# Two normalisation helpers of a three-block layer stack: the weight is multiplied before the statistics, the scaling after them is one operation a half

## The chip, the cores and the metric

The kernel runs on one core of a Trainium2 chip. The metric is the device time of one execution in microseconds, from several executions of the same program, of which the median is given. One execution was also recorded by the hardware profiler, and every row below is from that one. PE is the TensorE matmul engine (PEld its weight loads), DVE is VectorE, ACT is ScalarE, POOL is GpSimd, and SP issues DMAs.

## The reference, cut to what matters

A sequence of 512 positions with 1024 features goes through two layers of one kind and one of another. Each layer normalises, multiplies by weights, adds to the residual, and does so again for its feed-forward half:

```python
def rms_norm(x, g):
    y = x * rsqrt(mean(x * x, axis=-1, keepdims=True) + EPS)
    return y * g

def hybrid_layer(x, ...):              # twice
    u = rms_norm(x, g_mix_pre) @ w_in
    mix = concat([attention(u), conv(u), retention(u)]) @ w_out
    x = x + rms_norm(mix, g_mix_post)
    f = square(relu(rms_norm(x, g_mlp_pre) @ w_up)) @ w_down
    return x + rms_norm(f, g_mlp_post)

def second_block(h, ...):              # once
    proj = rms_norm(h, norm1_gain) @ w_in          # attention and a state-space branch
    h = h + (gated sum of both branches) @ w_out
    return h + glu_conv(rms_norm(h, norm2_gain) @ w_up) @ w_down
```

The row statistic of a norm is one number per position, the weight g one number per feature.

## The kernel before, in words

The 512 positions are four tiles t of 128; a tile's residual row block X[t] is two halves h of 128x512 floats in SBUF. All matrix products are made from high and low parts in fp32r (names ending in hi and lo), three matmuls for each. Weights come as one stream of 512 KB pieces (tile wraw); each is split by a cast to whi (ACT) and a subtraction to wlo (POOL or DVE).

Two helpers make the norms. `post_update(t, srcs, X, gpost)` takes the two halves of a product (from PSUM, or from the SBUF accumulators acc), squares each on ACT with an accumulated sum into the small tile st, adds the two sums on DVE, raises to the power -0.5 on POOL, and then on DVE, for each half, writes tmp = src * st * gain and adds tmp to X. `pre_norm(t, X, gpre)` takes the same statistic of X and writes, on DVE, hs = X * st * gain. `to_hT` then transposes hs on PE (matmuls with the identity cm), and a cast on ACT (hhi) and a subtraction on DVE (hlo) make the left operand of the next stage. In the trace hs and tmp both bear the name t, the weights gain, and the squares' unused output junk.

There are six sites. At the start, `pre_norm` is made for four tiles of the input. Then, twice, `finish` (after w_out: the first half's product p0[t] lies in PSUM, the second half is computed in a loop over t) and `finish_mlp` (after w_down: both halves are added into acc in a loop over t) each do `post_update`, `pre_norm` and the next tile's products in turn. Last, the second block's w_out loop does `pre_norm` alone. So there are 24 calls of `pre_norm` and 16 of `post_update`, 8 on PSUM halves and 8 on acc.

Behind each site the next stage begins with `f_split`: four products on the first 256 columns (tiles 0 and 1), then the same four on the other 256; `mid_start` puts the transposes of tiles 2 and 3 among the first ones. The next stage therefore can't begin before tile 1 is through its norms, transposes and split.

The order of the instructions is written out ahead of time. Every call is recorded by `Trace.add` with its dependences and a due time; `Trace.order` simulates the five engines with fixed costs (`cost`), takes on each engine the ready operation with the earliest due time within a window, gives out buffers (55 SBUF tiles of 128x512, four and four PSUM banks), chooses between engines for casts (`copy`) and subtractions (`sub`), and `issue` then emits that order. Its costs know nothing of one engine waiting for another's SBUF access. Each engine then executes in that order, so an instruction that waits holds all behind it on its engine. Since all is emitted from line 642, rows bear L642 and are told apart by tile names.

Of the kernel before, what the change touches and what calls it, by code (L numbers as in the profile page):

```python
# [13 lines left out]
AF = mybir.ActivationFunctionType  # L14
ALU = mybir.AluOpType
# [793 lines left out]
class Builder:  # L809
# [149 lines left out]
    def post_update(self, t, srcs, X, gpost):  # L959
        nc = self.nc  # L960
        st = self.st()
        for h in range(2):
            nc.scalar.activation(self.junk(), srcs[h], AF.Square, scale=1.0 / 32, accum_out=st[:, h:h + 1])
        nc.vector.scalar_tensor_tensor(st[:, 2:3], st[:, 0:1], EPS, st[:, 1:2], op0=ALU.add, op1=ALU.add)
        nc.gpsimd.tensor_tensor(st[:, 3:4], st[:, 2:3], self.mhalf[:, :1], op=ALU.pow)
        for h in range(2):
            tmp = self.s2()
            nc.vector.scalar_tensor_tensor(tmp, srcs[h], st[:, 3:4], gpost[h], op0=ALU.mult, op1=ALU.mult)
            nc.vector.tensor_tensor(X[t][h], X[t][h], tmp, op=ALU.add)

    def pre_norm(self, t, X, gpre):
        nc = self.nc
        st = self.st()
        for h in range(2):
            nc.scalar.activation(self.junk(), X[t][h], AF.Square, scale=1.0 / 32, accum_out=st[:, h:h + 1])
        nc.vector.scalar_tensor_tensor(st[:, 2:3], st[:, 0:1], EPS, st[:, 1:2], op0=ALU.add, op1=ALU.add)
        nc.gpsimd.tensor_tensor(st[:, 3:4], st[:, 2:3], self.mhalf[:, :1], op=ALU.pow)
        hs = []
        for h in range(2):
            tmp = self.s2()  # L980
            nc.vector.scalar_tensor_tensor(tmp, X[t][h], st[:, 3:4], gpre[h], op0=ALU.mult, op1=ALU.mult)
            hs.append(tmp)
        return hs

    def to_hT(self, t, hs):
# [1102 lines left out]
```

## Time and profile before

| | |
|---|---|
| median of 3 runs | 2135.91 us (2134.16 to 2139.28) |
| the profiled execution's own time | 2135.72 us |
| its span, first to last instruction | 2134.0 us |
| PE busy | 2036.2 us (95%) |
| DVE busy | 1362.7 us (64%) |
| ACT busy | 931.8 us (44%) |
| POOL busy | 727.8 us (34%) |
| mean granted TensorE clock | 0.990 |

Busy shares are means over the whole run. In a timeline row the number in square brackets is how long the engine was idle just before that row, and what ended the idle time; xN says that N instructions of one kind are merged in a row, and the time is then that of all N. PEclk in a table by stretches is the mean granted clock there, 1.00 being 2.4 GHz and 0.50 being 1.2 GHz.

### The profile page before, as it was taken

The numbers are of one execution on the slowest core, as the hardware profiler recorded it, in microseconds if no ns is written. First come the engines' busy times: TensorE is split into PE (matmuls) and PEld (weight loads), VectorE is DVE, ScalarE is ACT, GpSimd is POOL, SyncE is SP. The second block draws the span as 40 slices with busy tenths as digits, with TensorE's granted clock in tenths as the row PEclk, the third lists the DMA queues.
The fourth block names the chain that finished last, engine by engine and source line by source line (L and its number), as shares of the span: only waits on it lengthen the run. The fifth ranks groups of instructions, "written<-read, shape, count | busy, mean of one in ns | idle before, by whom it ended". The sixth has DMA issues, their size and how long they took to land. (4 is left out here: it accounts for less than half of the span.)

```text
span 2134.0 us, 27037 instructions
## 1 busy us (share of the span) xinstructions
PE 2036.2 (95%) x9964; PEld 1709.2 (80%) x9964; DVE 1362.7 (64%) x2127; ACT 931.8 (44%) x1527; POOL 727.8 (34%) x858
## 2 busy tenths in 40 slices
PE   7999889999999998899999998999999999999999
PEld 7987788778888977688888887677777788888887
DVE  5998795444457998563445473379888546655545
ACT  3377544222234376543233244457568224333322
POOL 3662367970004662300000035854553431000000
PEclk9999999999999999999999999999999999999999
DMA  5423333333242423222333354322324423333322
GB/s 181 129 60 119 109 103 130 111 117 99 79 126 90 129 72 116 79 90 89 98 90 108 99 186 139 91 85 65 98 82 146 164 88 100 99 99 99 97 81 79
DMA packets 85556, 225.16 MB, mean 106 GB/s; under 512 B 10416, under 2 KB 20400, under 8 KB 85424
## 3 DMA queue, kind: packets, MB, share of 16 engines
q1 hardware_dynamic: 85424, 223.43, 32.9%
q8 instruction: 79, 1.29, 0.3%
q14 instruction: 53, 0.43, 0.1%
HBM read 204.25 MB, written 19.14 MB: 105 GB/s over the span
## 5 line engine op out<-in xcount | busy, mean ns | idle before, releaser
L642 POOL TENSOR_TENSOR wlo<-wraw,whi 128x1024 fp32r<-128x1024 f32 (+1 forms) x156 | 367.1, 2361 | 1066.9 <-ACT whi L642 865.7
L642 ACT CAST whi<-wraw 128x1024 fp32r<-128x1024 f32 (+1 forms) x323 | 330.8, 1031 | 702.7 <-PE ps L642 617.8
L642 PE MATMUL ps<-hhi,whi 128*128 128x512 f32 (+1 forms) x1488 | 502.7, 367 | 8.7 <-DVE acc L642 2.8
L642 PE MATMUL ps<-hlo,whi 128*128 128x512 f32 (+1 forms) x1488 | 501.7, 367 | 6.8 <-DVE hlo L642 6.8
L642 PE MATMUL ps<-hhi,wlo 128*128 128x512 f32 (+1 forms) x1488 | 501.4, 366 | 0.4 <-DVE wlo L642 0.3
L642 PEld LDWEIGHTS ps<-hhi,whi 128*128 128x128 f32 x1488 | 273.5, 191 | 52.7 <-issue 5.1
L642 PEld LDWEIGHTS ps<-hlo,whi 128*128 128x128 f32 x1488 | 273.8, 192 | 49.3 <-DVE hlo L642 7.9
L642 PEld LDWEIGHTS ps<-hhi,wlo 128*128 128x128 f32 x1488 | 273.4, 191 | 43.4 <-DVE wlo L642 1.4
L642 DVE TENSOR_TENSOR wlo<-wraw,whi 128x1024 fp32r<-128x1024 f32 x178 | 224.6, 1263 | 109.2 <-ACT whi L642 109.1
L642 PE MATMUL ps<-whi,fhi 128*128 128x512 f32 x688 | 249.0, 391 | 5.1 <-DVE acc L642 2.8
L642 PE MATMUL ps<-whi,flo 128*128 128x512 f32 x688 | 249.3, 390 | 0.0
L642 PE MATMUL ps<-wlo,fhi 128*128 128x512 f32 x688 | 249.2, 391 | 0.0
L642 DVE TENSOR_TENSOR acc<-ps,acc 128x512 f32<-128x512 f32 x112 | 76.5, 687 | 153.0 <-PE ps L642 153.0
L642 PE MATMUL ps<-wlo,hhi 128*128 128x384 f32 (+1 forms) x448 | 157.6, 371 | 3.8 <-POOL wlo L642 3.8
L642 PE MATMUL ps<-whi,hhi 128*128 128x384 f32 (+1 forms) x448 | 155.7, 371 | 0.9 <-ACT whi L642 0.7
L642 PEld LDWEIGHTS ps<-whi,fhi 128*128 128x128 f32 x688 | 129.5, 188 | 32.6 <-DVE acc L642 3.2
L642 PE MATMUL ps<-whi,hlo 128*128 128x384 f32 (+1 forms) x448 | 155.3, 370 | 0.0
L642 PEld LDWEIGHTS ps<-whi,flo 128*128 128x128 f32 x688 | 129.7, 189 | 27.1
L642 PEld LDWEIGHTS ps<-wlo,fhi 128*128 128x128 f32 x688 | 129.8, 189 | 26.9
L642 POOL TENSOR_TENSOR st<-st,mhalf 128x1 f32<-128x1 f32 (+1 forms) x56 | 54.8, 980 | 194.0 <-DVE st L642 192.0
L642 DVE TENSOR_SCALAR t<-ps 128x512 f32<-128x512 f32 x64 | 44.1, 690 | 87.9 <-PE ps L642 87.9
L642 DVE TENSOR_TENSOR X<-ps,X 128x512 f32<-128x512 f32 x56 | 38.6, 689 | 91.7 <-PE ps L642 91.7
(249 smaller groups left out, 3247.5 us busy)
## 6 DMA issues: line engine op xcount, KB each, us to landing
wraw<-in_wst SPq DMA_DIRECT2D x302, 512.0 KB, 3.5
wraw<-in_wst SPq DMA_DIRECT2D x32, 384.0 KB, 3.1
gain<-in_gains SPq DMA_DIRECT2D x20, 256.0 KB, 4.3
X<-in_x SPq DMA_DIRECT2D x16, 256.0 KB, 5.4
xd<-X SPq DMA_DIRECT2D x16, 256.0 KB, 2.0
X<-xd SPq DMA_DIRECT2D x16, 256.0 KB, 5.5
gated<-t SPq DMA_DIRECT2D x16, 256.0 KB, 2.1
gate<-gated SPq DMA_DIRECT2D x16, 256.0 KB, 3.6
```

The source lines that it names most:

```text
L642: getattr(getattr(self.nc, e), m)(*[r(x) for x in op.args], **{k: r(v) for k, v in op.kw.items()})
```

## The change

In `post_update` each source half is multiplied by its weight into a new tile sg before the statistic, and after it one DVE operation a half adds sg * st to X. In `pre_norm` the weight is multiplied into hs before the statistic on DVE, and after it ACT scales hs in place by st.

```diff
     def post_update(self, t, srcs, X, gpost):
         nc = self.nc
         st = self.st()
+        sg = []
         for h in range(2):
+            sg.append(self.s2(name="sg"))
+            nc.vector.tensor_tensor(sg[h], srcs[h], gpost[h], op=ALU.mult)
             nc.scalar.activation(self.junk(), srcs[h], AF.Square, ...)
         nc.vector.scalar_tensor_tensor(st[:, 2:3], ...)
         nc.gpsimd.tensor_tensor(st[:, 3:4], ..., op=ALU.pow)
         for h in range(2):
-            tmp = self.s2()
-            nc.vector.scalar_tensor_tensor(tmp, srcs[h], st[:, 3:4], gpost[h], op0=ALU.mult, op1=ALU.mult)
-            nc.vector.tensor_tensor(X[t][h], X[t][h], tmp, op=ALU.add)
+            nc.vector.scalar_tensor_tensor(X[t][h], sg[h], st[:, 3:4], X[t][h], op0=ALU.mult, op1=ALU.add)

     def pre_norm(self, t, X, gpre):
         nc = self.nc
         st = self.st()
+        hs = []
         for h in range(2):
+            hs.append(self.s2())
+            nc.vector.tensor_tensor(hs[h], X[t][h], gpre[h], op=ALU.mult)
             nc.scalar.activation(self.junk(), X[t][h], AF.Square, ...)
         nc.vector.scalar_tensor_tensor(st[:, 2:3], ...)
         nc.gpsimd.tensor_tensor(st[:, 3:4], ..., op=ALU.pow)
-        hs = []
         for h in range(2):
-            tmp = self.s2()
-            nc.vector.scalar_tensor_tensor(tmp, X[t][h], st[:, 3:4], gpre[h], op0=ALU.mult, op1=ALU.mult)
-            hs.append(tmp)
+            nc.scalar.activation(hs[h], hs[h], AF.Copy, scale=st[:, 3:4])
         return hs
```

## Rows read from the trace of the kernel before

**Rows 1.** The page's first part: busy time, share of the span, instructions.
```profile
PE 2036.2 (95%) x9964; PEld 1709.2 (80%) x9964; DVE 1362.7 (64%) x2127; ACT 931.8 (44%) x1527; POOL 727.8 (34%) x858
```
**Rows 2.** Waits of PE, whole run: total us, times, longest us.
```profile
PE ps L642 <- DVE t L642: 19.6, 14, 2.8
PE ps L642 <- DVE hlo L642: 6.8, 5, 2.4
PE ps L642 <- ACT hhi L642: 1.9, 2, 1.5
```
**Rows 3.** Stretches around five sites: length, busy us of each engine, clock, DMA.
```profile
0.00:27.00 27.00, 13.94 (x90) 12.97 (x91) 16.57 (x22) 13.40 (x27) 13.12 (x12) 1.00 0.80 283
252.00:296.00 44.00, 35.13 (x205) 31.39 (x204) 38.34 (x74) 16.15 (x36) 24.30 (x22) 0.88 0.35 113
640.00:660.00 20.00, 16.66 (x97) 14.64 (x95) 18.82 (x23) 11.28 (x24) 12.87 (x8) 0.91 0.31 100
895.00:915.00 20.00, 14.39 (x82) 12.21 (x81) 19.58 (x28) 10.42 (x22) 8.89 (x7) 0.91 0.36 106
1260.00:1280.00 20.00, 16.60 (x125) 15.28 (x124) 18.36 (x27) 13.46 (x30) 14.22 (x9) 1.00 0.74 244
```
**Rows 4.** Timeline of PE at the sites: start, us, tiles, idle before.
```profile
7.55 1.94 PE L642 MATMUL ps<-cm,t 128*128 128x128 f32 x8 [7.55 <-DMA cm<-in_cmat]
...
14.61 1.11 PE L642 MATMUL ps<-cm,t 128*128 128x128 f32 x4 [1.65 <-DVE t L642]
...
21.43 0.30 PE L642 MATMUL ps<-cm,t 128*128 128x128 f32 x1 [1.51 <-DVE t L642]
...
263.84 1.12 PE L642 MATMUL ps<-cm,t 128*128 128x128 f32 x4 [2.76 <-DVE t L642]
...
649.24 0.66 PE L642 MATMUL ps<-cm,t 128*128 128x128 f32 x4 [1.30 <-DVE t L642]
...
899.64 0.66 PE L642 MATMUL ps<-cm,t 128*128 128x128 f32 x4 [1.75 <-DVE t L642]
...
907.52 0.63 PE L642 MATMUL ps<-cm,t 128*128 128x128 f32 x4 [2.13 <-DVE st L642]
...
1264.39 0.66 PE L642 MATMUL ps<-cm,t 128*128 128x128 f32 x4 [1.30 <-DVE t L642]
```
**Rows 5.** Timeline of DVE: an undisturbed pair, then two of those behind rows 4.
```profile
638.50 1.41 DVE L642 SCALAR_TENSOR_TENSOR t<-X,st,gain 128x512 f32<-128x512 f32 x2 [0.66 <-POOL st L642]
...
645.65 3.53 DVE L642 SCALAR_TENSOR_TENSOR t<-X,st,gain 128x512 f32<-128x512 f32 x2
...
903.86 3.51 DVE L642 SCALAR_TENSOR_TENSOR t<-X,st,gain 128x512 f32<-128x512 f32 x2
```
**Rows 6.** Timeline of POOL, 903 to 907 us.
```profile
903.28 0.55 POOL L642 TENSOR_TENSOR st<-st,mhalf 128x1 f32<-128x1 f32 x1 [4.24 <-DVE st L642]
903.99 2.83 POOL L642 TENSOR_TENSOR wlo<-wraw,whi 128x1024 fp32r<-128x1024 f32 x1 [0.16 <-ACT whi L642]
```
**Rows 7.** Groups by shape, whole run: busy us, mean ns, idle before.
```profile
L642 DVE SCALAR_TENSOR_TENSOR t<-X,st,gain 128x512 f32<-128x512 f32 x48 | 53.2, 1145 | 7.8 <-POOL st L642 6.2 <-DMA gain<-in_gains 1.6
...
L642 DVE TENSOR_TENSOR X<-X,t 128x512 f32<-128x512 f32 x32 | 21.7, 707 | 0.0
...
L642 DVE SCALAR_TENSOR_TENSOR t<-acc,st,gain 128x512 f32<-128x512 f32 x16 | 15.5, 1009 | 3.7 <-POOL st L642 3.7
...
L642 DVE SCALAR_TENSOR_TENSOR t<-ps,st,gain 128x512 f32<-128x512 f32 x16 | 11.5, 741 | 1.8 <-POOL st L642 1.8
...
L642 ACT ACTIVATE row<-row,st 128x512 f32<-128x512 f32 x12 | 8.5, 709 | 0.0
```
**Rows 8.** Operations that read gain: minimum, median, maximum ns.
```profile
L642 DVE SCALAR_TENSOR_TENSOR t<-X,st,gain x48: 735/750/2874, 6.6 to 1774.3; 128x512 f32<-128x512 f32 x48
...
L642 DVE SCALAR_TENSOR_TENSOR t<-ps,st,gain x16: 734/740/751, 254.3 to 913.0; 128x512 f32<-128x512 f32 x16
```
**Rows 9.** Timeline of DVE at the start.
```profile
6.57 1.50 DVE L642 SCALAR_TENSOR_TENSOR t<-X,st,gain 128x512 f32<-128x512 f32 x2 [1.55 <-DMA gain<-in_gains]
```

## The prediction

> **What bounds the kernel now.** First read the busy line [rows 1]: PE is busy 2036.2 of 2134.0 us, so at most 97.8 us of the span are idle PE, and no other engine comes near. What the norms can give is therefore in PE's idle time, and the next view is who ends it [rows 2]: DVE writing t (the normalised tile that PE transposes, but also other tiles of that name) 19.6 us, DVE writing hlo 6.8, ACT writing hhi 1.9. Third, the table by stretches says where [rows 3]. Length less PE busy is 13.06, 8.87, 3.34, 5.61 and 3.40 us for the start and the four ends of a layer half, 34.3 in all; 7.55 of the first is a load of the identity matrix [rows 4], so 26.7 us lie behind the norms. The last site, ahead of the final feed-forward, is not in the table because PE hardly waits there. In the four later stretches the reader is to see DVE: 38.3 of 44, 18.8, 19.6 and 18.4 of 20 us, against a mean of 64% over the run. The stage is bound by DVE's queue while the kernel is bound by PE. The granted clock there is 0.88, 0.91 and 0.91: a stretch at 1.2 GHz follows the idle time in three of the sites.
>
> Then the idle times one by one [rows 4]. Seven of them, 1.65, 1.51, 2.76, 1.30, 1.75, 2.13 and 1.30 us, sum 12.4, wait for the transposes' input. Behind these stands one pattern [rows 5]: the pair of operations t<-X,st,gain that ends pre_norm, 1.41 us when undisturbed, takes 3.5 us. One of the two is held for some 2.1 us, and POOL tells by what [rows 6]: the power that the pair waited for ends at 903.83, POOL takes the next subtraction wlo<-wraw,whi at 903.99, and the DVE pair that began at 903.86 has its second half stuck until POOL is done at 906.82. The 48 of that form have a median of 750 ns but a maximum of 2874 [rows 8], while the form that reads PSUM and gain never exceeds 751.
>
> **The change part by part.** Counts first. On DVE post_update goes from four operations a call to four, pre_norm from two to two. So DVE loses no work by count: before, 48, 32, 16 and 16 instructions cost 53.2 + 21.7 + 15.5 + 11.5 = 101.9 us [rows 7]. What moves is the order along the chain and who is exposed to POOL.
>
> A. The end of pre_norm leaves DVE. On ACT the nearest row with a per-partition operand from SBUF is row<-row,st, 0.71 us [rows 7]; I take that for the scaled copy. A pair is 1.42 us against 1.41 on DVE, so an undisturbed chain gains nothing by it, but the held 2.1 us go. In post_update, the two additions, 0.71 each by the mean [rows 7], leave the chain between the power and the next squares, since the new operation is both multiply and add. So a tile is 1.4 us earlier at its second statistic, less what the moved weight multiplies take: those of X are ready only with X itself, and one of 0.7 us can stand ahead of the small addition of the sums. Net 0.7 to 1.4. With 2.1 from the held pair, 2.8 to 3.5 us are to be had where 12.4 us of idle pieces are 1.3 to 2.8 each, so each could vanish. Bounds 0 and -12.4; I take three quarters, -9.3, since POOL's power and ACT's own queue remain.
>
> B. The idle behind hhi and hlo, 8.7 us [rows 2], ends with the split, whose subtraction is queued on DVE. DVE there loses held time: 53.2 us less 48 x 0.75 is 17.2 us of waiting in the pairs of pre_norm over the run. Some of it returns in the new operations (D). Bounds 0 and -8.7; I take a third, -2.9.
>
> C. The clock. 12% of 44 us and 9% of 20 twice are 8.9 us of full-clock time not granted [rows 3]. PE had idle time in those stretches too, so 8.9 is the upper bound; if two of three low stretches shorten or go, about a third, -3.0, is likely.
>
> D. What the new operations add. The X operation reads sg and X, both in SBUF, directly behind POOL's power, where before on the 8 tiles of finish the operation read PSUM and was never held [rows 8]. At the mean excess of the pre_norm form, 1145 - 750 = 395 ns [rows 7, 8], 16 operations cost 6.3 us of DVE; half of these tiles (0 and 1) are ahead of the next stage's first matmul, so about +2. Bounds: 0, and one held operation of 2.1 us on each of the 8 tiles, +17. The Trainium skill, page "SBUF — State Buffer", section "SBUF: two separate sides", says that VectorE with two SBUF inputs and GpSimd take one port pair as an exclusive lock for a whole instruction, whoever starts first. The held pairs of 3.5 us agree with it; by that rule alone the new X operation is as exposed as the old pair of pre_norm, and D would stand near its upper bound.
>
> E. ACT gets 48 copies of 0.71, 34 us, about 5.7 at a site. In the stretches ACT is busy 16.2 of 44 and 10.4 to 13.5 of 20 [rows 3], so the work is hidden as such; but a copy waits on ACT for POOL's power, and queued behind it are the next tile's squares, the casts of weights to whi and the casts hhi. If each of tiles 0 and 1 at four sites loses one ACT operation of 0.71 that is 8 x 0.71 = +5.7; if none, 0. I take +2.
>
> F. The start. The gains land at 6.57 us [rows 9], after the first statistic; so there the weight multiply is not ahead of it, and the first tile pays a multiply of 0.7 (the 0.71 again) and a copy of 0.71 where it paid one operation of 0.75. Bounds 0 and +0.9 with the handover; +0.5.
>
> The tiles sg and hs live longer, which can hold back an early allocation in the ordering, and PSUM banks come free earlier as sg, not PSUM, is read last. I price both at zero. Sum: -9.3 - 2.9 - 3.0 + 2 + 2 + 0.5 = -10.7. The profiled execution took 2135.72 us, its span 2134.0; the median of the runs is 2135.91, so the profile stands for them. 2135.7 - 10.7 = 2125.0 us.
>
> **The rivals.** *The waits only move, no change.* DVE's work by count is the same and it is 92 to 98% busy in the last three finishing stretches, so the subtraction for hlo comes as late as now. Then A yields only about a quarter, -3, B and C nothing, D to F +2: 2135. For it: the count. Against it: the pairs that PE waits for are the very ones that are held.
>
> *The held operation moves with the chain: slower.* Right behind each power POOL starts the next subtraction, and the X operation, which both later squares and the second power wait for, is held at the place of the old pair; all that follows in the tile slides, and ACT, waiting in order for the second power, holds weight casts as well. Price: +17 (D) and +5.7 (E) against A's -9.3, and B and C nothing: +13, 2149. It decides from the point at which the tiles held on the path, at 2.1 each, outweigh A and E's remainder: (9.3 - 2)/2.1, more than three of eight. For it, rows 6; against it, POOL has a subtraction ready only after ACT has cast the weights, and where the sites' post_update reads acc, mean 1009 against 740 for the form never held [rows 7, 8], most pairs ran free.
>
> *All idle time behind the norms goes.* A, B and C at their bounds with D to F nil: -30, 2106.
>
> **How the numbers follow.** Forecast 0.57, with its own range of 2114 to 2131; waits move 0.25; held X operations 0.13; all gone 0.05. Each step of the fixed order elsewhere can shift as well: of the 97.8 us idle, 63.5 are outside the five stretches, and a reshuffle of a few per cent of it is 2 or 3 us either way. A measurement tells about 0.2% from no change, 4.3 us here. Faster by more: 0.60 (most of the forecast, all of the last rival and a little of the second); within: 0.25; slower: 0.15. The range for 8 in 10 is 2112 to 2141.
>
> **What would show it.** After the change the pairs of about 3.5 us should be gone from the operations in front of the transposes, which should follow ACT copies of about 0.7 us; PE's waits for the normalised tile and for hlo together should fall from 26.4 to some 15 us, and the stretches at 0.88 and 0.91 should rise. D shows as a mean of the new X operation well above 0.75 us. The prediction is wrong if PE's idle time in the five stretches stays near 34 us, with waits for hlo or hhi in the place of t, or if ACT's queue ends most of it; or if idle time elsewhere changes by as much as here.

## The result, and the profile after

The changed kernel takes 2147.02 us (median of 5 runs, 2146.03 to 2150.51) where the kernel before, on the same chip, takes 2134.42 (2133.47 to 2139.28): a ratio of 1.0051 as recorded, 95% interval 1.0039 to 1.0063 (the two medians alone give 1.0059; the recorded ratios below differ from those of the medians by up to 0.0008 as well). It is slower by 12.6 us. The forecast was 2125.0 in a range of 2112 to 2141; the time lies outside, on the side of the rival called "the held operation moves with the chain" (2149).

The busy line of the changed kernel, against [rows 1]:

```profile
PE 2045.0 (95%) x9964; PEld 1712.3 (80%) x9964; DVE 1361.1 (63%) x2133; ACT 962.6 (45%) x1572; POOL 726.4 (34%) x859
```

The span grew from 2134.0 to 2145.3 us. Of these 11.3 us only 2.5 are more idle time of PE (100.3 against 97.8); 8.8 are the same 9964 matmuls taking longer. The mean granted clock says why: 0.990 before, 0.986 after. With the two levels 2.4 and 1.2 GHz counting as 1.00 and 0.50, a stretch at 1.2 GHz takes from the mean just the half of its length that it can lose. So what the mean misses, times the span, is the time lost at most: 2134.0 x 0.010 is 21.3 us before, 2145.3 x 0.014 is 30.0 us after, 8.7 more.

Next, what PE waits for in the changed kernel, whole run: total us, times, longest us. It answers to [rows 2].

```profile
PE ps L642 <- DVE hlo L642: 19.7, 7, 5.4
...
PE ps L642 <- ACT t L642: 16.5, 5, 8.7
PE ps L642 <- POOL wlo L642: 7.0, 5, 2.2
...
PE ps L642 <- DVE t L642: 3.9, 1, 3.9
...
PE ps L642 <- ACT hhi L642: 1.6, 2, 1.3
```

The 3.9 us behind DVE's t are one piece at 401.83 us, in front of ps<-whi,fhi: another tile of that name (2.3 us at that place before). The normalised tile is now waited for behind ACT. At sites 2 to 4 that wait is gone; it is left at the start (0 to 27 us), before and after:

```profile
PE ps L642 <- DVE t L642: 5.5, 3, 2.4
...
PE ps L642 <- ACT t L642: 9.4, 2, 8.7
```

where PE had waited another 7.5 us for the identity first, and at site 1 (252 to 296 us before, 254.6 to 298.6 after), where it rose:

```profile
PE ps L642 <- DVE t L642: 3.3, 2, 2.8
...
PE ps L642 <- ACT t L642: 6.8, 2, 6.6
```

The wait for hlo rose from 6.8 to 19.7. The stretches around the five sites, each moved by the delay that it begins with, against [rows 3] (length, busy us of each engine, clock, DMA):

```profile
0.00:27.00 27.00, 14.17 (x82) 12.70 (x83) 12.06 (x23) 17.46 (x34) 12.46 (x12) 1.00 0.80 283
254.60:298.60 44.00, 32.70 (x199) 29.30 (x198) 39.21 (x80) 21.50 (x44) 28.44 (x26) 0.88 0.36 124
641.50:661.50 20.00, 14.57 (x73) 11.99 (x72) 19.01 (x22) 10.73 (x23) 12.72 (x8) 0.87 0.34 117
901.90:921.90 20.00, 14.40 (x83) 12.41 (x82) 16.45 (x27) 15.55 (x32) 6.31 (x7) 0.83 0.31 106
1266.80:1286.80 20.00, 14.17 (x94) 12.87 (x93) 18.46 (x25) 12.20 (x26) 12.87 (x7) 0.91 0.75 236
```

PE has 41.0 us without work in these 131 us (34.3 before), and the clock is 0.87, 0.83 and 0.91 where it was 0.91, 0.91 and 1.00. PE's timeline shows the idle pieces one by one, against [rows 4] (start, us, tiles, idle before):

```profile
8.69 1.12 PE L642 MATMUL ps<-cm,t 128*128 128x128 f32 x4 [8.69 <-ACT t L642]
...
274.01 1.97 PE L642 MATMUL ps<-cm,t 128*128 128x128 f32 x8 [6.63 <-ACT t L642]
...
290.13 0.39 PE L642 MATMUL ps<-hlo,whi 128*128 128x256 f32 x1 [2.58 <-DVE hlo L642]
...
661.32 0.58 PE L642 MATMUL ps<-hlo,whi 128*128 128x256 f32 x1 [3.81 <-DVE hlo L642]
...
916.31 0.58 PE L642 MATMUL ps<-hlo,whi 128*128 128x256 f32 x1 [4.24 <-DVE hlo L642]
...
1281.38 0.58 PE L642 MATMUL ps<-hlo,whi 128*128 128x256 f32 x1 [5.36 <-DVE hlo L642]
```

Pieces of 1.3 to 2.8 us have become fewer and longer ones, up to 6.6 us behind the start. The one at 661.32 explains itself on DVE and POOL (timelines of the two engines, 651 to 662 us), against [rows 5, 6]:

```profile
651.10 0.55 POOL L642 TENSOR_TENSOR st<-st,mhalf 128x1 f32<-128x1 f32 x1
651.54 0.68 DVE L642 TENSOR_TENSOR hlo<-ps,hhi 128x512 fp32r<-128x512 f32 x1
651.61 7.90 POOL L642 TENSOR_TENSOR wlo<-wraw,whi 128x1024 fp32r<-128x1024 f32 x3
652.14 5.17 DVE L642 SCALAR_TENSOR_TENSOR X<-sg,st,X 128x512 f32<-128x512 f32 x2
...
657.23 3.44 DVE L642 TENSOR_TENSOR t<-X,gain 128x512 f32<-128x512 f32 x2
...
660.59 0.68 DVE L642 TENSOR_TENSOR hlo<-ps,hhi 128x512 fp32r<-128x512 f32 x1
```

POOL ends the power that the X operations wait for and goes straight on with three weight subtractions, 7.90 us. The two X operations behind that power take 5.17 us and the two weight multiplies 3.44. Behind these four on DVE stands the second half of tile 1's hlo, which PE needs. Before, at the same place, POOL made the same burst (three subtractions, 7.95 us), but the kernel before had both halves of hlo ahead of the pair that was held:

```profile
651.95 1.27 DVE L642 TENSOR_TENSOR hlo<-ps,hhi 128x512 fp32r<-128x512 f32 x2
...
654.27 3.52 DVE L642 SCALAR_TENSOR_TENSOR t<-acc,st,gain 128x512 f32<-128x512 f32 x2 [0.53 <-POOL st L642]
```

The same pattern stands at 1271 to 1281 us. At site 3 (the 4.24 us before 916.31) no norm operation is held; there a weight subtraction of 1.21 us, X operations of 1.42 and weight multiplies of 1.29 stand on DVE ahead of hlo, unheld. So at sites 2 to 4 PE waits for what stands in front of hlo, and at two of them the hold makes that longer. Last, the groups of the changed kernel by shape (busy us, mean ns, idle before), against [rows 7]:

```profile
L642 DVE TENSOR_TENSOR t<-X,gain 128x512 f32<-128x512 f32 x48 | 44.2, 952 | 5.2 <-DMA gain<-in_gains 4.9
L642 DVE SCALAR_TENSOR_TENSOR X<-sg,st,X 128x512 f32<-128x512 f32 x32 | 33.1, 1074 | 5.0 <-POOL st L642 4.9
L642 ACT ACTIVATE t<-t,st 128x512 f32<-128x512 f32 x48 | 32.5, 717 | 13.5 <-POOL st L642 13.5
...
L642 ACT ACTIVATE junk<-ps 128x512 bf16<-128x512 f32 x16 | 9.5, 594 | 23.5 <-DVE sg L642 22.2 <-PE ps L642 1.3
```

And the durations of the two that are held on DVE, against [rows 8] (minimum, median, maximum ns):

```profile
L642 DVE TENSOR_TENSOR t<-X,gain x48: 677/685/2845, 6.1 to 1780.2; 128x512 f32<-128x512 f32 x48
...
L642 DVE SCALAR_TENSOR_TENSOR X<-sg,st,X x32: 739/752/2859, 257.8 to 1284.6; 128x512 f32<-128x512 f32 x32
```

Busy time beyond count times median is taken as the held time. After: 33.1 - 32 x 0.752 = 9.0 and 44.2 - 48 x 0.685 = 11.3, together 20.3 us. Before, by [rows 7, 8]: 17.2 in pre_norm's pairs and, taking the 0.740 of the PSUM form as undisturbed, 3.7 in the form that reads acc, together 20.9. So the held time was hardly less. It stands in front of something else.

**Steps by stretch.** Both traces hold 9964 matmuls, so how much later the matmul of one number starts can be read off at the ends of stretches. The order differs in places (at 1951 numbers the changed kernel runs a matmul of other tiles), so a number stands for the same progress, not always for the same product. The stretches reach from about 0 to 28, 226 to 306, 630 to 678, 890 to 938, 1240 to 1288 and 1724 to 1812 us of the run before; ends some 10 us further out or in change the sums over the six sites by up to 1 us. In us, each column the growth within that stretch against the profiled run of before (site 5 is the last one, ahead of the final feed-forward); the kernels below the first row are those of the experiments:

| kernel | start | site 1 | site 2 | site 3 | site 4 | site 5 | six sites | elsewhere |
|---|---|---|---|---|---|---|---|---|
| changed | 1.0 | 0.8 | 5.4 | -0.1 | 3.6 | 2.0 | +12.7 | -1.4 |
| e1 post_update alone | -0.1 | -1.7 | 3.5 | 0.7 | 1.6 | 0.0 | +4.0 | -0.2 |
| e2 pre_norm alone | 1.2 | 0.6 | 1.7 | 2.4 | 1.4 | 2.0 | +9.3 | -9.5 |
| e3 before, other window | 0.0 | -1.1 | 0.0 | 1.5 | 0.1 | 0.0 | +0.5 | +1.2 |
| e9 changed, other window | 1.3 | 0.1 | 5.5 | 0.0 | 3.7 | 2.0 | +12.7 | +2.0 |
| e5 scaling on DVE | -0.2 | -6.6 | 0.2 | 0.1 | -0.4 | 2.4 | -4.6 | +0.6 |
| e7 before, POOL kept free | -0.5 | 0.7 | 2.8 | -0.1 | 3.6 | 0.0 | +6.5 | -4.4 |
| e8 changed, POOL kept free | 2.2 | -5.9 | 3.1 | -5.8 | -0.6 | 2.0 | -5.0 | -7.2 |
| f1 changed, split first | 1.4 | -1.4 | 0.4 | -4.1 | 3.3 | 2.0 | +1.6 | -4.9 |
| f2 before, split first | -0.1 | -1.8 | 3.2 | 0.4 | 3.0 | 0.0 | +4.7 | -6.2 |
| f3 changed, hold known | 2.3 | -3.3 | 1.6 | -4.7 | -1.6 | 0.7 | -5.0 | -58.8 |
| f4 before, hold known | -2.9 | -1.4 | 3.7 | 1.0 | 2.2 | 0.6 | +3.2 | -45.3 |
| f5 as f3, other window | 1.0 | -1.0 | 1.6 | -4.9 | -1.4 | 0.7 | -4.0 | -40.5 |
| f6 as f4, other window | -3.0 | -1.9 | 3.7 | 1.0 | 2.1 | 0.6 | +2.5 | -40.3 |

The loss is at the sites. "Elsewhere" moves by up to 9.5 us in the rows of the planner of before, with no reason found in the norms; this is taken for chance of the order. The last four rows, of a planner that knows the hold, move there by 40 us and more, which is another matter.

### The profile page after: what moved, and what is told of

Its sections match the earlier page's. It is cut to its first block, busy times and chain, and to the rows that moved or that the text cites. A ratio compares the mean times of both kernels' runs of the same rounds, so it can differ in the third digit from the quotient of the medians.

```text
span 2145.3 us, 27084 instructions
## 1 busy us (share of the span) xinstructions
PE 2045.0 (95%) x9964; PEld 1712.3 (80%) x9964; DVE 1361.1 (63%) x2133; ACT 962.6 (45%) x1572; POOL 726.4 (34%) x859
## 3 DMA queue, kind: packets, MB, share of 16 engines
q8 instruction: 79, 1.29, 0.2%
## 5 line engine op out<-in xcount | busy, mean ns | idle before, releaser
L642 POOL TENSOR_TENSOR wlo<-wraw,whi 128x1024 fp32r<-128x1024 f32 (+1 forms) x157 | 372.2, 2378 | 1069.1 <-ACT whi L642 823.7
L642 ACT CAST whi<-wraw 128x1024 fp32r<-128x1024 f32 (+1 forms) x320 | 328.1, 1031 | 720.0 <-PE ps L642 645.0
L642 PE MATMUL ps<-hlo,whi 128*128 128x512 f32 (+1 forms) x1488 | 502.7, 368 | 19.8 <-DVE hlo L642 19.7
L642 PE MATMUL ps<-hhi,whi 128*128 128x512 f32 (+1 forms) x1488 | 505.3, 371 | 5.9 <-ACT whi L642 2.2
L642 PE MATMUL ps<-hhi,wlo 128*128 128x512 f32 (+1 forms) x1488 | 502.1, 368 | 2.3 <-POOL wlo L642 1.8
L642 PEld LDWEIGHTS ps<-hlo,whi 128*128 128x128 f32 x1488 | 275.1, 193 | 63.6 <-DVE hlo L642 21.7
L642 PEld LDWEIGHTS ps<-hhi,whi 128*128 128x128 f32 x1488 | 275.0, 193 | 51.6 <-ACT whi L642 4.5
L642 PEld LDWEIGHTS ps<-hhi,wlo 128*128 128x128 f32 x1488 | 274.2, 192 | 45.8 <-POOL wlo L642 2.1
L642 DVE TENSOR_TENSOR wlo<-wraw,whi 128x1024 fp32r<-128x1024 f32 x177 | 221.9, 1255 | 113.0 <-ACT whi L642 110.9
L642 PE MATMUL ps<-whi,fhi 128*128 128x512 f32 x688 | 249.8, 391 | 6.5 <-DVE t L642 3.9
L642 PE MATMUL ps<-wlo,fhi 128*128 128x512 f32 x688 | 249.9, 391 | 0.0
L642 PE MATMUL ps<-whi,flo 128*128 128x512 f32 x688 | 249.2, 390 | 0.0
L642 DVE TENSOR_TENSOR acc<-ps,acc 128x512 f32<-128x512 f32 x112 | 76.6, 688 | 151.1 <-PE ps L642 151.1
L642 PE MATMUL ps<-wlo,hhi 128*128 128x384 f32 (+1 forms) x448 | 158.6, 372 | 5.2 <-POOL wlo L642 5.2
L642 PE MATMUL ps<-whi,hhi 128*128 128x384 f32 (+1 forms) x448 | 155.3, 370 | 2.6 <-DVE vlo L642 2.6
L642 PEld LDWEIGHTS ps<-whi,fhi 128*128 128x128 f32 x688 | 129.7, 189 | 34.1 <-DVE t L642 4.3
L642 PE MATMUL ps<-whi,hlo 128*128 128x384 f32 (+1 forms) x448 | 156.5, 369 | 0.0
L642 PEld LDWEIGHTS ps<-whi,flo 128*128 128x128 f32 x688 | 129.5, 188 | 26.9
L642 PEld LDWEIGHTS ps<-wlo,fhi 128*128 128x128 f32 x688 | 129.6, 189 | 26.6
L642 POOL TENSOR_TENSOR st<-st,mhalf 128x1 f32<-128x1 f32 (+1 forms) x56 | 50.3, 907 | 190.2 <-DVE st L642 185.5
L642 DVE TENSOR_SCALAR t<-ps 128x512 f32<-128x512 f32 x64 | 44.2, 691 | 101.6 <-PE ps L642 101.6
L642 PEld LDWEIGHTS ps<-wlo,hhi 128*128 128x128 f32 x448 | 84.3, 190 | 15.9 <-POOL wlo L642 7.2
```

The lines of the kernel that those rows point to most:

```text
L642: getattr(getattr(self.nc, e), m)(*[r(x) for x in op.args], **{k: r(v) for k, v in op.kw.items()})
```

## The experiments

All ratios are against the kernel before, run on the same chip beside the experiment, with 95% intervals.

**The two halves, and the chance of the order.** e1 has the new post_update with the old pre_norm, e2 the reverse. e3 and e9 change only the planner's window, in the kernel before and in the changed one:

```diff
-    WINDOW = 25160.0
+    WINDOW = 25000.0
```

> The new post_update with the old pre_norm (no early multiply of X, no copies on ACT). Theory: the slowdown at the ends of the feed-forward halves (+5.4 and +3.2 us by the position of PE's matmuls) comes from the X operation, which is held by POOL's subtractions right behind the power, and from the early multiply that stands with it in front of hlo on DVE. Then post_update alone is 3 to 6 us slower than before, with the X pair again near 5 us at the end of a feed-forward half, and the start and the last site (+1.0 and +2.0) are as before. Rival 1, ACT's queue with the 48 copies is the cause: then this kernel is within 2 us of before or faster. Rival 2, any new order of the instructions is worth some us either way: no number, but steps at places that the edit does not touch are as large as those at the sites.

> The old post_update with the new pre_norm. Theory: the start and the last site keep their +1.0 and +2.0 us (no post_update there); at the four other sites the held pair goes from in front of the transposes, and the early multiply costs some of it back: in all -3 to +4 us against before. Rival 1 (ACT's copies): +8 us or more. Rival 2: no number.

> The kernel before with the window of the ordering at 25000 instead of 25160 ns: the same instructions in a slightly other order. Theory: within 2 us of before. Rival 2 (order alone): 4 us or more away, in either direction.

> The changed kernel with the window of the ordering at 25000 instead of 25160 ns, the counterpart of the same edit on the kernel before. Theory: the loss belongs to the change, so the six sites are again 9 to 16 us longer than before by the position of PE's matmuls. Rival (order by chance): the sites come out below 5 us longer.

e1: 2139.80 us, 1.0017 (1.0008 to 1.0027). e2: 2137.10, 1.0003 (0.9993 to 1.0013). e3: 2136.36, 1.0004 (0.9993 to 1.0015). e9: 2149.47, 1.0064 (1.0049 to 1.0079). At the six sites the halves cost +4.0 and +9.3, and 13.3 together is near the +12.7 of the whole. Neither half alone is a gain there. e1, e3 and e9 came out as their theories had them. e2's time lies in the range of its theory, but only because 9.5 us went elsewhere, where no second window was run to test it; by its sites it is at the price of rival 1. A shifted window moves the sites by 0.5 in the kernel before and leaves the loss of the changed one at 12.7, so the loss at the sites is no chance of the order, as far as one other window tells.

**The shared PSUM bank.** In post_update the square and the new multiply read the same bank, the planner lets one engine at a time work on a PSUM bank, and ACT sat idle 22.2 us behind sg (the group junk<-ps above; before, the same squares had waited 17.5 us, for PE). e4 records the square first:

```diff
+            nc.scalar.activation(self.junk(), srcs[h], AF.Square, ...)
             nc.vector.tensor_tensor(sg[h], srcs[h], gpost[h], op=ALU.mult)
-            nc.scalar.activation(self.junk(), srcs[h], AF.Square, ...)
```

> The changed kernel with the square recorded ahead of the weight multiply in post_update, so that where both read the same PSUM bank, the square no longer waits for the multiply (ACT idle until DVE sg: 22 us in the changed kernel). Theory: some 1 us each at the two ends after w_out, the feed-forward ends unchanged: 8 to 11 us slower than before. Rival 3, the shared PSUM bank is the main cost: at most 5 us slower than before.

2146.82 us, 1.0049 (1.0034 to 1.0064), the six sites +15.0 (in its slowest execution, 2150.27 us, which is the one profiled). The planner gave DVE the same order, instruction for instruction, and ACT still waits 22.2 us for sg. So it matters nothing which of the two is recorded first, and the wait itself was not taken away; what it costs stays untested. As a repeat the run bears out the loss.

**The scaling on DVE in place of ACT.**

```diff
-            nc.scalar.activation(hs[h], hs[h], AF.Copy, scale=st[:, 3:4])
+            nc.vector.tensor_scalar(hs[h], hs[h], st[:, 3:4], None, op0=ALU.mult)
```

> The changed kernel with the scaling of hs after the statistic on DVE (a one-source multiply) instead of a copy on ACT. Theory (held operations and the early multiply in front of hlo on DVE): no better than the changed kernel, 8 to 16 us slower than before, since DVE gets work and the early multiply stays. Rival 1 (ACT's queue with the 48 copies): at most 4 us slower than before, the steps at the sites mostly gone.

> The changed kernel with the scaling on DVE, and the window at 25000. Theory: the gain against the changed kernel belongs to the engine, so this is 10 us or more faster than the changed kernel at the same window, and the six sites stay between -8 and +2 us against before. Rival (order by chance): within 5 us of the changed kernel at the same window.

e5: 2131.89 us, 0.9985 (0.9975 to 0.9995). e10, the same with window 25000: 2133.18, 0.9991 (0.9981 to 1.0000). This refutes the theory stated for e5 and is what rival 1 had; e10 came out as expected. The six sites go from +12.7 to -4.6 and -4.4: 7.4 us of it at site 1, 9.2 at sites 2 and 4, where in e5 no X operation is held (the hold falls on a multiply into sg instead). At site 1 ACT's timeline of the changed kernel has:

```profile
272.65 0.60 ACT L642 ACTIVATE junk<-ps 128x512 bf16<-128x512 f32 x1 [2.62 <-DVE sg L642]
...
273.24 1.32 ACT L642 ACTIVATE t<-t,st 128x512 f32<-128x512 f32 x2
```

and DVE's, what sg stood behind:

```profile
267.26 3.44 DVE L642 TENSOR_TENSOR t<-X,gain 128x512 f32<-128x512 f32 x2
270.62 1.28 DVE L642 TENSOR_TENSOR hlo<-ps,hhi 128x512 fp32r<-128x512 f32 x2
271.82 0.14 DVE L642 SCALAR_TENSOR_TENSOR st<-st 128x1 f32<-128x1 f32 x1
271.88 0.68 DVE L642 TENSOR_TENSOR sg<-ps,gain 128x512 f32<-128x512 f32 x1
```

The copy of one tile stands on ACT behind another tile's square; the square waits for sg; sg stands on DVE behind a held weight multiply. PE's 6.63 us before 274.01 come out of that chain. ACT is not short of time there (21.5 of 44 us busy), it is short of order. But this piece is not what e5 gains most by: PE still waits there, now for DVE,

```profile
271.58 1.94 PE L642 MATMUL ps<-cm,t 128*128 128x128 f32 x8 [5.18 <-DVE t L642]
```

and the two waits for hlo behind it (1.88 and 2.58 us in the changed kernel) are the larger part of what went.

e11 leaves the copies recorded as they are and makes them short:

```diff
-            nc.scalar.activation(hs[h], hs[h], AF.Copy, scale=st[:, 3:4])
+            nc.scalar.activation(hs[h][:, :64], hs[h][:, :64], AF.Copy, scale=st[:, 3:4])
```

> The changed kernel with copies on ACT over 64 of the 512 columns; the other 448 columns of hs stay without the statistic. The copies wait for POOL's power as before and stand in ACT's queue, but take some 0.3 us instead of 0.72. Theory a, the time of the copies on ACT is what loses: within 4 us of before or faster. Theory b, the wait for the power in ACT's queue is: still 7 us or more slower than before.

2140.40 us, 1.0021 (1.0012 to 1.0031), the six sites +4.1. It is 5.9 us slower than before, between the two theories. The copies still take 346 ns of 717, so this does not split the loss between duration and waiting; it says that shorter copies are worth 8.6 us at the sites.

**The multiply taken out.** e6 leaves the 48 multiplies by gpre out and scales X itself:

```diff
-            nc.vector.tensor_tensor(hs[h], X[t][h], gpre[h], op=ALU.mult)
...
-            nc.scalar.activation(hs[h], hs[h], AF.Copy, scale=st[:, 3:4])
+            nc.scalar.activation(hs[h], X[t][h], AF.Copy, scale=st[:, 3:4])
```

> The changed kernel without the 48 multiplies of X by the weight: pre_norm leaves gpre out, and ACT writes the scaled copy of X straight to hs. The copies on ACT stay, DVE loses the early multiplies. Theory: most of the loss at the sites goes: between 6 us faster and 5 us slower than before; the X pair is still held. Rival 1 (ACT's queue): still 7 us or more slower, since ACT does all that it did in the changed kernel.

2118.59 us, 0.9919 (0.9905 to 0.9934), 15.7 us faster than before and so beyond the theory's range; the six sites -5.3, and 11.4 of the gain lie elsewhere. So the 48 multiplies, 44.2 us of DVE of which 11.3 are held, are worth 18 us at the sites.

**POOL's subtractions taken out of the way.** In e7 (before) and e8 (changed) the first 14 weight pieces of each finishing site are subtracted on DVE, so that POOL has next to nothing but powers there (the main lines):

```diff
-            nc.sub(lo[:, :n], t[:, :n], hi[:, :n].bitcast(F32), b.wbias)
+            nc.sub(lo[:, :n], t[:, :n], hi[:, :n].bitcast(F32), None if b.nopool > 0 else b.wbias)
+            b.nopool -= 1
```

> The kernel before with the subtractions for wlo kept off POOL for the 14 weight pieces from the beginning of each of the four finishing stages (they go to DVE, 1.2 us each). No other operation of POOL there, so DVE is held less, but has more to do. Reference for the next run: 0 to 12 us slower than before.

> The changed kernel with the same pieces kept off POOL. Theory: without POOL's subtractions nothing holds the X pair, so against the run before (the kernel before with the same pieces off POOL) the four finishing sites together are from 4 us shorter to 3 us longer by the position of PE's matmuls, where the changed kernel was 9.7 longer; the start and the last site stay at +1 and +2. Rival 1 and the early multiply's place in DVE's order without holding: the four sites stay 6 us or more longer.

> The changed kernel with the scaling on DVE and the wlo subtractions of the 14 pieces a site kept off POOL. Theory (the three causes act together, and either removal breaks the chain): little more than the better of the two alone, 8 to 14 us faster than before. Rival (each removes a loss of its own): 18 us or more faster than before.

e7: 2136.92 us, 1.0011 (1.0001 to 1.0020). e8: 2123.12, 0.9943 (0.9928 to 0.9958). With POOL kept free the change is worth -13.8 us, 11.5 of them at the sites (-5.0 against +6.5). The four finishing sites of e8 are 16.2 us shorter than those of e7, far beyond the 4 that were expected. In both runs no norm operation of sites 2 to 4 takes over 1.1 us, so the hold is gone there; at site 1 some still take 1.2 to 1.8. And the hold is not all: at site 2 of e8 PE waits

```profile
647.99 0.58 PE L642 MATMUL ps<-hlo,whi 128*128 128x256 f32 x1 [5.86 <-DVE hlo L642]
```

where three weight subtractions (3.50 us) now stand on DVE ahead of the unheld chain. e12 adds DVE's scaling to e8: 2119.35, 0.9923 (0.9904 to 0.9941). The two remedies gain 2.4 and 11.2 us alone and 15.2 together, a little more than its theory allowed and less than the rival's 18.

So the loss goes when POOL's burst, the multiply, or the copy on ACT is taken away, and each of these edits also gives a new order. That left two readings: the chain of the norms is late in any order, or only the order is wrong.

**The order.** f1 gives hlo and hhi of tiles 0 and 1 due times 6 us earlier, after all due times are set, and changes nothing else by hand; the planner then orders all around them anew. f2 does so in the kernel before. The edit in words, not in its own lines:

```diff
+        # when the due times are set, for every operation of split() in to_hT with t < 2
+        op.due -= 6000.0
```

> The changed kernel, with the casts hhi and subtractions hlo of tiles 0 and 1 given due times 6 us earlier, so that on DVE hlo stands ahead of the X operations and weight multiplies of later tiles. Theory a (the loss is the order: held X operations and multiplies, 8.6 us at the second site, stand in front of tile 1's hlo): the steps at the second and fourth site (+5.4, +3.6) go to within 1 of none or below, PE's waits for hlo fall from 19.7 to under 10, and the time is 2132 to 2139. Theory b (what stands in front of hlo does not matter: the chain itself, statistic, power, X, is late): waits for hlo become waits for t or hhi and the time stays within 4 us of the changed kernel's, 2143 to 2151.

> The same earlier due times in the kernel before, as the control. There hlo is waited for 6.8 us only. Theory a: it gains at most 4 us, 2130 to 2136, so the change costs less than 6 once both have their splits first. Theory b: both kernels move alike and the distance of some 12 us between them stays.

f1: 2131.49 us, 0.9981 (0.9972 to 0.9991). f2: 2135.57, 1.0003 (0.9994 to 1.0013). With the split ahead, a loss of 12.6 us is a gain of 3.4, and the kernel before is as it was (in f2 6.2 us gained elsewhere hide 4.7 lost at the sites, where PE's longest pieces are now 6.92 and 5.25 us behind t). Both times are as theory a had them, f1's by half a us below its range. PE's waits for hlo in f1:

```profile
PE ps L642 <- DVE hlo L642: 5.5, 3, 2.4
```

and its second site, in the timelines of POOL and DVE:

```profile
645.09 11.62 POOL L642 TENSOR_TENSOR wlo<-wraw,whi 128x1024 fp32r<-128x1024 f32 x4 [0.98 <-POOL st L642]
...
649.28 2.37 DVE L642 TENSOR_TENSOR sg<-acc,gain 128x512 f32<-128x512 f32 x1
...
651.57 0.68 DVE L642 TENSOR_TENSOR hlo<-ps,hhi 128x512 fp32r<-128x512 f32 x1
...
652.17 2.29 DVE L642 TENSOR_TENSOR sg<-acc,gain 128x512 f32<-128x512 f32 x1
...
654.38 2.35 DVE L642 SCALAR_TENSOR_TENSOR st<-st 128x1 f32<-128x1 f32 x1
...
657.25 1.42 DVE L642 SCALAR_TENSOR_TENSOR X<-sg,st,X 128x512 f32<-128x512 f32 x2 [0.53 <-POOL st L642]
```

POOL's burst is even longer, and DVE is held as much, but hlo has come through, and the site's step is 0.4 instead of 5.4. The fourth site kept its +3.3 against what was expected: there tile 1's hlo stood behind a held 128x1 addition and a held multiply (2.35 and 2.33 us). Against the changed kernel's 12.7, f1 has 1.6 at the sites: 5.0 less at site 2, 4.0 at site 3, 2.2 at site 1. The wait behind ACT's copies at site 1 is untouched:

```profile
274.41 1.97 PE L642 MATMUL ps<-cm,t 128*128 128x128 f32 x8 [6.62 <-ACT t L642]
```

so the loss went without it. hhi was moved along with hlo, and no run moves one of the two alone.

f3 and f4 let the planner know the hold: an operation of DVE with two inputs in SBUF (or a tensor_scalar or copy from SBUF to SBUF) is not started until POOL's has ended, and the other way round. The main lines:

```diff
-                    wait = 0.0
+                    wait = held[{"vector": "gpsimd", "gpsimd": "vector"}[e]] if pair(op, e) else 0.0
...
+                    if pair(op, e):
+                        held[e] = op.end
```

> The changed kernel, ordered by a planner that holds a DVE operation with two SBUF inputs until a POOL operation has ended, and the other way round. Theory a (the order was written blind to the hold): it puts other work in the held time, loses no more than 4 us against before or gains, 2122 to 2138. Theory b (the held chain is bound by the data): 2143 to 2152. The reshuffle of everything else is worth 3 us either way.

> The kernel before with the same planner: it says what of the run before's gain is the change's. Theory a: it gains less than the changed kernel does from the planner, 2128 to 2136. Theory b: both gain or lose alike, within 4 us of each other's difference to their own kernel.

> The changed kernel ordered with the hold known, and the planner's window 25000 instead of 25160, which shifts the order and nothing else. Theory a (the change is worth 8 us at the six sites once the hold is known, and the other 13 of the 21 us between the two planned kernels are chance of the order in the second block): 2072 to 2086, with the sites again 5 us or more below the unchanged order's. Theory b (all 21 us are the change's): 2070 to 2076.

> The kernel before, ordered with the hold known, with window 25000. Theory a: 2080 to 2096, and the sites again about +3 against the run before, so that the distance to the changed kernel at the sites stays near 8 us while that elsewhere does not. Theory b: 2090 to 2097, the distance stays 21 us in all.

f3: 2072.53 us, 0.9706 (0.9692 to 0.9721). f4: 2093.55, 0.9803 (0.9787 to 0.9819). With window 25000, f5: 2092.09, 0.9805 (0.9789 to 0.9821), and f6: 2098.75, 0.9833 (0.9819 to 0.9848). All four gain 36 to 62 us, nearly all of it outside the sites. For f3 and f4 that is far more than was expected; f5 and f6, whose ranges were set after these two, came out slower than either of their theories (2092.09 against at most 2086, 2098.75 against at most 2097). Between the kernels, the change gains 21.0 us in one pair and 6.7 in the other; at the six sites it is 8.2 (-5.0 against +3.2) and 6.5 (-4.0 against +2.5). That part stays in both windows and is put down to the change; the 13.5 us more that f3 gains over f4 elsewhere are put down to chance of the order, since the other pair has only 0.2. The busy lines of f3 and f4:

```profile
PE 2020.0 (98%) x9964; PEld 1699.2 (82%) x9964; DVE 1323.1 (64%) x2151; ACT 961.6 (46%) x1573; POOL 696.7 (34%) x840
...
PE 2029.2 (97%) x9964; PEld 1707.8 (82%) x9964; DVE 1323.3 (63%) x2151; ACT 934.0 (45%) x1527; POOL 679.8 (32%) x837
```

With more instructions than under the planner of before, DVE is busy 38 to 39 us less in each kernel, and PE's idle time is 50.2 and 62.7 us where it was 100.3 and 97.8. This fits DVE's instructions being held less over the whole run, not only in the norms. The groups of f3 by shape (a few added lines make L661 of L642):

```profile
L661 DVE TENSOR_TENSOR t<-X,gain 128x512 f32<-128x512 f32 x48 | 36.6, 791 | 6.2 <-DMA gain<-in_gains 5.6 <-DMA X<-in_x 0.4
...
L661 DVE SCALAR_TENSOR_TENSOR X<-sg,st,X 128x512 f32<-128x512 f32 x32 | 27.7, 907 | 4.3 <-POOL st L661 4.3
```

and of f4, whose pairs are still those of before:

```profile
L661 DVE SCALAR_TENSOR_TENSOR t<-X,st,gain 128x512 f32<-128x512 f32 x48 | 44.3, 956 | 7.3 <-POOL st L661 7.0 <-DMA gain<-in_gains 0.3
```

The means fall from 952 and 1074 to 791 and 907, and before's from 1145 to 956, but not to their medians; what is still held is seldom in front of hlo. PE's waits for hlo in f3:

```profile
PE ps L661 <- DVE hlo L661: 1.6, 2, 0.8
```

and in f4:

```profile
PE ps L661 <- DVE hlo L661: 4.1, 5, 1.3
```

f3 is the fastest kernel of the study, with the change in it as it was. Site 1 still has its piece behind ACT's copies (7.51 us).

## Why the prediction was wrong, step by step

**What bounds the kernel** was read rightly: PE's idle time behind the norms, with DVE's queue as the limit of the stage. The figure that should have warned is in the same view: DVE 92 to 98% busy in three stretches [rows 3], so that whatever is held there delays what stands behind it.

**A, the held pair leaves PE's path (-9.3).** Right at three sites, wrong at one. PE's waits for t or st were 1.3, 4.7 and 2.2 us at sites 2 to 4 and are gone; at site 1 they went from 3.3 to 6.8, behind ACT's copies. At the start the 13.0 us for the identity and t became 9.4, but 1.6 for whi and 1.8 for wlo came in their place. That is -8.3 in all, near the forecast's size, and partly by luck, since 3.6 of it brought nothing. The seven pieces of the prediction also leave out one of 2.36 us at the start, at 11.85.

**B, the idle behind hlo and hhi (-2.9).** This is the step that failed, and with it the sign. The prediction let "a third" of that idle go since DVE's held time would shrink. It measured +12.6 (19.7 + 1.6 against 6.8 + 1.9). The held time stayed (20.9 before, 20.3 after), because POOL's subtractions stayed: only its place changed. The text said that "the order along the chain" moves, but never asked where hlo then stands on DVE among the moved operations. The planner, which counts 0.6 to 0.7 us for each of them, put four in front of it at sites 2 and 4, and they took 8.6 us. f1 shows that this place is the cause at sites 2 and 3: with the split moved ahead, PE's waits for hlo are 5.5 us and the loss is gone in the sum. At site 4 f1 did not bring hlo forward enough (a step of 3.3); there the step is gone only with POOL kept free (-0.6 in e8), the scaling on DVE (-0.4 in e5) or the hold known (-1.6 in f3).

**C, the clock (-3.0).** Wrong with B: +8.7 by the mean clocks. The stretches at 0.91, 0.91 and 1.00 went to 0.87, 0.83 and 0.91 with their fewer and longer idle pieces. So 6.7 us more idle time in the five stretches goes with steps of 12.7 at the sites, and the rival's sum, too, had the clock at nothing.

**D, the new X operation (+2).** Mis-sized. Its mean is 1074 ns, 322 over its median; the 32 of them lose 9.0 us of DVE, where the 6.3 of the prediction were for 16. By place it decides: at sites 2 and 4 it is the operation held right behind the power, as the rival had it, and the pair there takes 5.17 and 5.19 us where an undisturbed one takes 1.41. The prediction took the mean row of an operation that stood elsewhere in the sequence. The Trainium skill, page "SBUF — State Buffer", section "SBUF: two separate sides", has VectorE with two SBUF inputs and GpSimd take one port pair exclusively for a whole instruction. By that rule the new operation is as exposed as the old pair, and the trace agrees (5.17 us for two beside 7.90 of POOL's).

**E, 48 copies on ACT (+2).** Their duration was right (717 ns measured, 709 assumed). "The work is hidden as such" was true of ACT's busy time and wrong of its order, as site 1 shows; with the scaling on DVE the sites are 17 us better (e5), with short copies 8.6 (e11). This is no fixed price of the copies, since f3 keeps them and gains.

**F, the start (+0.5)** measured +1.0, its upper bound being 0.9. The last site was given no price and cost 2.0 in the changed kernel and in e2, e8, e9 and f1, 2.4 with the scaling on DVE, 0.5 with short copies and 0.7 in f3 and f5; why was not followed.

**The rivals.** "The held operation moves with the chain", 2149 at a chance of 0.13, is what happened by the place of the hold (the X operations behind the power) and nearly by its price (+13; the sites measured +12.7). But what slid was not chiefly the rest of the same tile, as it had it: PE lost by the hlo of tile 1 that stood on DVE behind the held operations. Its sum came out right with the wrong parts, which is luck: +17 for D was too much, and B's +12.6 and the clock's +8.7 stood at nothing. What the prediction held against it (most pairs ran free where acc is read) was a mean over the order of before, which the change rewrites.

**What would make it wrong** was named: PE's idle time in the five stretches near 34 with waits for hlo in the place of t. It is 41.0, and that is the wait.

What stays open: the wait of ACT for sg in a shared PSUM bank was not taken away alone, the losses at the start and the last site (1.0 and 2.0) were not traced to a cause, hhi was not moved without hlo, and where outside the norms the planner that knows the hold gains its 40 us was not looked into.

## What to carry to other kernels

Where one engine holds another, moving an operation does not remove the hold while the holder keeps its work: look for what will stand behind the held operation in its new place, and put the operations that the bounding engine waits for ahead of it. Where the order of instructions is computed, give the planner the hold before judging an edit of the kernel: the same change cost 12.6 us under an order blind to it and gained 7 and 21 us in two orders that knew it, and that knowledge alone was worth 41 and 37 us in the kernel before. Price an idle piece of PE together with the stretch at the lower clock that may go with it.

## What the runs showed of the hardware that was not expected

- In f1 a run of four POOL subtractions back to back (11.62 us) let through about one held DVE operation for each: two multiplies of 2.37 and 2.29 us and a 128x1 addition of 2.35. The small addition was held as long as the large multiplies, though it takes 0.15 us undisturbed. An operation that reads PSUM (hlo, 0.68 us) passed between them at its usual time.
- A multiply by one number per partition with a single SBUF input, 128x512 floats, has a median of 0.48 us on DVE (e5) and a mean of 0.72 on ACT (the changed kernel). e5's mean is 657 ns and its longest 2.64 us, so it is held at times as well. An undisturbed pair in e5:

```profile
661.63 0.88 DVE L642 TENSOR_SCALAR t<-t,st 128x512 f32<-128x512 f32 x2
```
